# Time credited for the matrix engine's extra products, and convolution statistics that add on VectorE

## The chip, the cores and the metric

The kernel runs on one core of a Trainium2 chip. The metric is the device time of one execution in microseconds (us). The kernel before takes 1073.52 us, the median of three runs (1072.88 to 1074.54). Its engines are PE (TensorE, with the weight load PEld beside it), VectorE (DVE), ScalarE (ACT), GpSimd (POOL) and SyncE (SP), whose queue issues most transfers.

## The reference

Two layers of a decoder step for 288 tokens: 256 of a prompt and 32 of a sample (8 sequences of 4 tokens) that have a paged cache of 256 past positions. Everything is float32. One layer computes

```python
g_cols, u_pool, u_conf, u_sc, q, k, v, qi, ki, wi = split_cols(x @ w_in)
a_out = pool_mixer(u_pool)                                   # windowed means, group mix
cv = causal_dwconv(ga * sigmoid(gb), 31 taps) + conv_b       # 256 channels
b_out = silu(layer_norm(cv, conv_ln_g, conv_ln_b))           # mean and variance over channels
c_out = sb * causal_dwconv(sc_ * sh, 3 taps)
d_out = attend(rope(q), rope(k), v, rope(qi), rope(ki), wi)  # indexer scores, top-k, attention
gates = sigmoid(g_cols)                                      # four gates of 1024 channels
merged = sum of gates[i] * (branch_i @ w_br_i)
x1 = layer_norm(ALPHA * x + merged @ w_o)
r = ALPHA * x1 + (silu(hg) * hu) @ w_ffn_out                 # hg, hu = x1 @ w_ffn_in
y = layer_norm(r + (pe @ w_pe) * sigmoid(r @ w_pg))
```

The attention keeps, for each query, the 64 best keys by the indexer's score (relu of qi.ki, weighted by wi) and softmaxes over those.

## The kernel before

Activations lie feature-major, 128 features x 288 tokens. The weights are 2448 tiles of 128x128 that are streamed in 306 groups of 8. For each group a transfer brings 512 KB (wraw), ScalarE rounds them (whi, L264), VectorE subtracts (wlo = wraw - whi, L271), and each tile is used by three matmuls: whi by the high part of the activations, whi by the low part, wlo by the high part (L292 to L294; L318, L322 and L324 where several outputs grow side by side). A group keeps PE busy for 24 x 0.132 = 3.17 us. At the first tile of a group, `W` (L277) issues the rounding for the group three ahead and the subtraction for the group two ahead, and then calls `side` (L205): a tick.

Everything else of the mixers is side work: tasks written as generators (index_prompt, index_sample, attn_prompt, attn_sample, sconv, pool, conv). A tick gives each of two budgets, VectorE 1.96 us and ScalarE 2.3 us, on top of what was overdrawn:

```python
self.left[i] = min(self.left[i], 0.0) + self.budget[i]
```

Then ready tasks are stepped in turn while the budgets that they need are above zero. `yield d, a` takes declared times from the two budgets, `yield n` sleeps n ticks, and `yield VECTOR` or `BOTH` sets which budgets the task needs. The conv task is of low priority: it gets only what the others leave. Each engine executes in the order in which it was issued, so what a tick issues stands on VectorE behind one subtraction and ahead of the next. A product that a task issues on PE stands there between two weight groups, and nothing is debited or credited for its time.

PE's outputs go to two pools of four banks: `mm` for the projections, `ax` for the side work. After the q, k, v and short-conv projections come the pool projection, the gates 0 and 2 (one group per product; sigmoid on ScalarE, L1063), then the branches pool and sconv (two tiles per product, four products per group; VectorE multiplies by the gate, L1075 and L1078), then gates 1 and 3 and the branch of the attention. The side work runs in ticks 7 to 64 of layer 0 and 161 to 218 of layer 1; the branches pool and sconv start near tick 44 and 198.

The lines that matter later: conv's taps L684 (60 multiplies per layer), its products and reductions for the sample L690 and L693, its mean L704 and variance L714; index_prompt's copy of ki (L759), the two sleeps around it, its logits L777 and the top-k L748 and L752; the attention's logits L834, its Exp L851, the scaling by the reciprocal sum L858, transposes L870, output L882; index_sample's products L945 and L947 and its final mask addition L960; the pool mixer's L629 to L633.

Of the kernel before, what the change touches and what calls it, by code (L numbers as in the profile page):

```python
# [13 lines left out]
AF = mybir.ActivationFunctionType  # L14
# [100 lines left out]
class Builder:  # L115
# [103 lines left out]
    def cost(self, d, a):  # L219
        self.left[0] -= d  # L220
        self.left[1] -= a

    def finish(self, t):
        n = 0
# [445 lines left out]
    def conv(self):  # L670
        nc = self.nc
        ce, w = self.ce, self.par("conv_w")
        cv = yield from self.get_b([128, 2, N])
        bias = self.par("conv_b")
        es = [ce[:, c, 30 + TP:].rearrange("p (b w) -> p b w", b=NB) for c in range(2)]
        yield VECTOR
        for j in range(31):
            for c in range(2):
                wj = w[:, 31 * c + j:31 * c + j + 1]
                o, e = cv[:, c, :TP], ce[:, c, j:j + TP]  # L680
                if j == 0:
                    nc.vector.tensor_scalar(o, e, wj, bias[:, c:c + 1], op0=OP.mult, op1=OP.add)
                else:
                    nc.vector.scalar_tensor_tensor(o, e, wj, o, op0=OP.mult, op1=OP.add)  # L684
                yield 0.49, 0
        pr = yield from self.get_b([128, NB, TS, 31])
        for c in range(2):
            e = es[c]
            e = bass.AP(tensor=e.tensor, offset=e.offset, ap=[list(e.ap[0]), [34, NB], [1, TS], [1, 31]])
            nc.vector.tensor_tensor(pr, e, w[:, None, None, 31 * c:31 * c + 31].to_broadcast([128, NB, TS, 31]),  # L690
                                    op=OP.mult)
            yield 1.1, 0
            nc.vector.tensor_reduce(bt(cv[:, c, TP:]), pr, axis=AX.X, op=OP.add)  # L693
            yield 1.1, 0
            nc.vector.tensor_scalar(cv[:, c, TP:], cv[:, c, TP:], bias[:, c:c + 1], None, op0=OP.add)
            yield 0.1, 0
        yield BOTH
        self.free()
        self.free()
        yield 1  # L700
        mu, var = yield from self.get_ax(2)
        mu, var = mu[:, :N], var[:, :N]
        for c in range(2):
            nc.tensor.matmul(mu, self.c("o1024"), cv[:, c], start=c == 0, stop=c == 1)  # L704
        sq = [self.s(), self.s()]
        for c in range(2):
            nc.vector.scalar_tensor_tensor(cv[:, c], mu, -4.0, cv[:, c], op0=OP.mult, op1=OP.add)
            yield 0.4, 0
        for c in range(2):
            nc.scalar.activation(sq[c], cv[:, c], AF.Square)  # L710
        yield 0, 0.8
        yield 1
        for c in range(2):
            nc.tensor.matmul(var, self.c("o1024"), sq[c], start=c == 0, stop=c == 1)  # L714
        sd = self.s()
        nc.scalar.activation(sd, var, AF.Sqrt, bias=self.c("eps"), scale=4.0)
        yield 0, 2.0
        yield 1
        self.free_ax(2)
        rs = self.s()  # L720
        nc.vector.reciprocal(rs, sd)
        yield 2.0, 0
        g, b = self.par("cg"), self.par("cb")
        t = [self.s(), self.s()]
        for c in range(2):
            nc.vector.tensor_tensor(cv[:, c], cv[:, c], rs, op=OP.mult)
            yield 0.4, 0
        for c in range(2):
            nc.vector.tensor_scalar(cv[:, c], cv[:, c], g[:, c:c + 1], b[:, c:c + 1], op0=OP.mult, op1=OP.add)
            yield 0.4, 0  # L730
        for c in range(2):
            nc.scalar.activation(t[c], cv[:, c], AF.Sigmoid)
            yield 0, 0.45
        yield 1
        for c in range(2):
            nc.vector.tensor_tensor(cv[:, c], cv[:, c], t[c], op=OP.mult)
            yield 0.4, 0
        self.br["conv"] = yield from self.parts(cv)
# [17 lines left out]
    def index_prompt(self):  # L756
# [1 line left out]
        yield 2  # L758
        nc.scalar.activation(self.ki[64:], self.ki[:64], AF.Copy)  # L759
        yield 0, 0.33  # L760
        yield 2
        wp = self.sb.tile([128, 2, 4], F32, name="wp", tag="wp", bufs=1)
        a = yield from self.get_ax()
        for i in range(2):
# [5 lines left out]
        for i in range(2):  # L770
# [4 lines left out]
            for h in range(4):  # L775
                r = slice(64 * (h % 2), 64 * (h % 2) + 64)
                nc.tensor.matmul(a[h % 2][:, h // 2], self.qi[r, h // 2, 128 * i:128 * (i + 1)], self.ki[r, :n],  # L777
                                 start=True, stop=True)
            for e in range(2):
                nc.scalar.activation(rl[:, e::2], a[e], AF.Relu, scale=0.0625)  # L780
                yield 0, 0.3 + n / 600
# [19 lines left out]
    def attn_prompt(self):  # L801
# [5 lines left out]
        for i in range(3):  # L807
            rows = 128 if i < 2 else NS
            a = yield from self.get_ax()
            for c in range(4):  # L810
                nc.tensor.transpose(a[:rows, 128 * c:128 * (c + 1)], self.v[:, c, 128 * i:128 * i + rows], ident)
            nc.scalar.activation(vt[:, i] if i < 2 else vs, a[:rows], AF.Copy)
            self.free_ax()
            yield 0, 0.65
# [5 lines left out]
        for i in range(2):  # L820
# [6 lines left out]
            for h1 in range(0, 8, 2 * hb):  # L827
# [4 lines left out]
                for h in range(h1, h1 + 2 * hb):  # L832
                    r = slice(64 * (h % 2), 64 * (h % 2) + 64)
                    nc.tensor.matmul(a[h % 2][:, (h - h1) // 2], self.q[r, h // 2, 128 * i:128 * (i + 1)],  # L834
                                     self.k[r, h // 2, :n], start=True, stop=True)
                yield 1
                hs = slice(h1, h1 + 2 * hb)
                for e in range(2):
# [23 lines left out]
            for kc in range(i + 1):  # L862
                pt = yield from self.get_b([128, 8, 128])
                pts.append(pt)
                for h0 in range(0, 8, 4):
                    a = yield from self.get_ax()
                    v = a.rearrange("p (h q) -> p h q", h=4)
                    for h in range(h0, h0 + 4):
                        lg = lgs[h // (2 * hb)]
                        nc.tensor.transpose(v[:, h - h0], lg[:, hb * (h % 2) + h % (2 * hb) // 2,  # L870
                                                             128 * kc:128 * (kc + 1)], ident)
                    nc.scalar.activation(pt[:, h0:h0 + 4], v, AF.Copy)
                    self.free_ax()
                    yield 0, 0.65
# [4 lines left out]
            for c in range(4):  # L879
                for kc in range(i + 1):  # L880
                    for s in range(2):
                        nc.tensor.matmul(o[64 * s:64 * s + 64, c], vt[:, kc, 128 * c + 64 * s:128 * c + 64 * s + 64],  # L882
                                         pts[kc][:, 2 * c + s], start=kc == 0, stop=kc == i)
            self.free(len(pts))
            w = slice(128 * i, 128 * (i + 1))
            nc.scalar.activation(dp[0][:, :, w], o, AF.Copy)
# [41 lines left out]
    def index_sample(self):  # L928
# [15 lines left out]
        for p in range(4):  # L944
            nc.tensor.matmul(a[32 * p:32 * p + 32, :NK], self.qibd[:, p].rearrange("p r h t -> p (r h t)"),  # L945
                             self.kx[:, p], start=True, stop=True)
        nc.tensor.matmul(a[:, 288:288 + NS], self.c("hsel")[:4], self.wi[:, TP:], start=True, stop=True)  # L947
        rl = self.sb.tile([128, NK], F32, name="rls", tag="rls", bufs=1)
        nc.scalar.activation(rl, a[:, :NK], AF.Relu, scale=0.0625)
        yield 0, 0.4  # L950
# [4 lines left out]
        yield 2  # L955
        a = yield from self.get_ax()
        nc.tensor.matmul(a[:NS, :NK], ws, rl, start=True, stop=True)
        sc = self.sb.tile([NS, NK], F32, name="scs", tag="scs", bufs=1)
        nc.scalar.activation(sc[:, :TP], a[:NS, :TP], AF.Copy)
        nc.vector.tensor_tensor(sc[:, TP:], a[:NS, TP:NK], self.c("vb")[:NS], op=OP.add)  # L960
# [9 lines left out]
    def attn_sample(self):  # L970
# [12 lines left out]
        for f in range(2):  # L983
# [7 lines left out]
            for c in range(4):  # L991
                for j in range(4):
                    nc.tensor.matmul(a[32 * j:32 * j + 32, :NK],  # L993
                                     self.qbd[:, c, 4 * f + j].rearrange("p h t -> p (h t)"),
                                     kt[j][:, :, c], start=False, stop=c == 3)
            yield 1
            st = self.sb.tile([128, 3], F32, name="sts", tag="sts", bufs=2)
            nc.vector.tensor_reduce(st[:, 0:1], a[:, :NK], axis=AX.X, op=OP.max)
# [29 lines left out]
            for kc in range(2):  # L1028
                for j in range(4):
                    nc.tensor.matmul(a[32 * j:32 * j + 32], pt[:, kc, 32 * j:32 * j + 32], vc[j][:, kc].rearrange("p c k -> p (c k)"),  # L1030
                                     start=False, stop=kc == 1)
            m = yield from self.get_b([128, 512])
            nc.scalar.activation(m, a, AF.Copy, scale=st[:, 2:3])
            self.free_ax()
# [3 lines left out]
            for c in range(4):  # L1038
                nc.tensor.transpose(a[:, 128 * c:128 * (c + 1)], m[:, 128 * c:128 * (c + 1)], ident)
            self.free()  # L1040
            w = slice(TP + 16 * f, TP + 16 * f + 16)
            own = []
            for s in range(2):
# [432 lines left out]
```

## Time and profile before

| | |
|---|---|
| median of 3 runs | 1073.52 us |
| the profiled execution's own time | 1073.4 us |
| its span | 1071.5 us |
| PE busy | 1055.5 us, 98%, 8078 matmuls |
| VectorE busy | 763.2 us, 71%, 1319 instructions |
| ScalarE busy | 564.2 us, 53%, 950 instructions |
| GpSimd busy | 157.1 us, 15% |
| granted PE clock, mean | 0.997 of full speed (2.4 GHz) |
| read from memory | 182.49 MB, 175 GB/s with the writes |

The span is from the first to the last recorded instruction; 1.9 us of the execution lie outside it. PE is the engine that is nearly always busy. Matmuls are pipelined: a record of 0.29 us starts 0.13 us after the one before, so progress is read from start to start. Rows of a timeline can merge several instructions of a kind (x4).

### The profile page before, as it was taken

To read this page: it belongs to the slowest core of one execution; us is meant where nothing else is said; L and a number is where in the kernel's file an instruction comes from. 1 tells how busy PE (TensorE), PEld (TensorE's weight loads), DVE (VectorE), ACT (ScalarE), POOL (GpSimd) and SP (SyncE) were. 2 spreads that over 40 slices of the span, in tenths; PEclk is the share of its full clock that TensorE was granted. 3 is DMA by queue.
4 is the path that set the end of the run, shared out by engine and by line. 5 is a ranking of instruction groups with operands and counts; after the bars stand their busy time and mean duration, and the time that the engine had idled before them with its cause. 6 is when DMAs were issued, how large, how long until landed. Compare 5 with 4: busy or idle time off the path is not lost.

```text
span 1071.5 us, 20583 instructions
## 1 busy us (share of the span) xinstructions
PE 1055.5 (98%) x8078; PEld 1022.4 (95%) x8078; DVE 763.2 (71%) x1319; ACT 564.2 (53%) x950; POOL 157.1 (15%) x177
## 2 busy tenths in 40 slices
PE   9999999999999999999999999999999999999996
PEld 8999989899999999999999999898999999999996
DVE  5898869668785565544789888786688756555456
ACT  4886446554564444434578665554645644443344
POOL 0530003005500000000425100030055000000004
PEclk9999999999999999999999999999999999999998
DMA  8577646554455555544555766465453545554541
GB/s 304 168 247 213 201 144 227 197 167 147 150 164 172 157 171 168 174 157 169 161 183 164 264 190 216 122 225 205 139 169 128 186 158 170 171 171 159 171 143 45
DMA packets 61778, 188.57 MB, mean 176 GB/s; under 512 B 7602, under 2 KB 12274, under 8 KB 61682
## 3 DMA queue, kind: packets, MB, share of 16 engines
q1 hardware_dynamic: 60546, 183.55, 52.8%
q0 software_dynamic: 992, 3.57, 1.0%
q8 instruction: 63, 1.03, 0.4%
q14 instruction: 33, 0.27, 0.1%
q10 hardware_dynamic: 144, 0.15, 0.1%
HBM read 182.49 MB, written 4.75 MB: 175 GB/s over the span
## 4 chain that ended last, share of the span: by engine, by line
PE 90%; DVE 4%; ACT 2%; issue 1%; DMA 1%; POOL 1%; SPq 1%; POOLq 0%; DVEq 0%; ACTq 0%
PE mm L292 25%; PE mm L293 25%; PE mm L294 24%; PE mm L322 2%; PE mm L324 2%; PE mm L318 2%; DVE wlo L271 1%; DMA wraw<-in_w_dram 1%; POOL b L374 1%; PE ax L293 1%; PE ax L294 1%; PE ax L292 1%; DVE b L684 1%; PE ax L993 1%; PE ax L1030 1%
## 5 line engine op out<-in xcount | busy, mean ns | idle before, releaser
L271 DVE TENSOR_TENSOR wlo<-wraw,whi 128x1024 fp32r<-128x1024 f32 (+1 forms) x309 | 385.7, 1251 | 161.6 <-issue 80.8
L292 PE MATMUL mm<-xh,whi 128*128 128x288 f32 x1536 | 455.5, 297 | 1.0 <-DVE s L1078 1.0
L293 PE MATMUL mm<-xl,whi 128*128 128x288 f32 x1536 | 453.1, 295 | 0.0
L294 PE MATMUL mm<-xh,wlo 128*128 128x288 f32 x1536 | 452.9, 295 | 0.2 <-DVE wlo L271 0.2
L264 ACT ACTIVATE whi<-wraw 128x1024 fp32r<-128x1024 f32 (+1 forms) x309 | 322.7, 1047 | 160.8 <-PE mm L293 80.7
L292 PEld LDWEIGHTS mm<-xh,whi 128*128 128x128 f32 x1536 | 288.8, 188 | 9.3 <-issue 7.3
L294 PEld LDWEIGHTS mm<-xh,wlo 128*128 128x128 f32 x1536 | 288.6, 188 | 0.6 <-DVE wlo L271 0.6
L293 PEld LDWEIGHTS mm<-xl,whi 128*128 128x128 f32 x1536 | 288.8, 188 | 0.3
L292 PE MATMUL mm<-b,whi 128*128 128x288 f32 x576 | 171.5, 298 | 1.9 <-DVE m L1075 1.9
L293 PE MATMUL mm<-b,whi 128*128 128x288 f32 x576 | 169.9, 295 | 0.0
L294 PE MATMUL mm<-b,wlo 128*128 128x288 f32 x576 | 169.5, 294 | 0.0
L292 PEld LDWEIGHTS mm<-b,whi 128*128 128x128 f32 x576 | 107.9, 187 | 2.8 <-DVE m L1075 2.6
L294 PEld LDWEIGHTS mm<-b,wlo 128*128 128x128 f32 x576 | 108.5, 188 | 0.0
L293 PEld LDWEIGHTS mm<-b,whi 128*128 128x128 f32 x576 | 108.1, 188 | 0.2
L1079 POOL TENSOR_TENSOR m<-m,s 128x288 f32<-128x288 f32 x32 | 37.7, 1209 | 268.5 <-DVE s L1078 268.5
L343 POOL TENSOR_TENSOR b<-xf 128x288 f32<-128x288 f32 x4 | 4.9, 1215 | 443.0 <-DVE xf L1230 434.4
L1203 ACT ACTIVATE b<-s 128x288 fp32r<-128x288 f32 x44 | 19.2, 444 | 92.3 <-DVE s L1198 92.3
L684 DVE SCALAR_TENSOR_TENSOR b<-b,prm 128x256 f32<-128x256 f32 x120 | 58.9, 539 | 0.1
L1198 DVE TENSOR_TENSOR s<-s,mm 128x288 f32<-128x288 f32 x40 | 18.0, 454 | 50.6 <-PE mm L294 50.6
L1063 ACT ACTIVATE xf<-mm 128x288 f32<-128x288 f32 x32 | 13.2, 411 | 53.9 <-PE mm L294 53.8
L1063 ACT ACTIVATE g<-mm 128x288 f32<-128x288 f32 x32 | 13.2, 411 | 47.9 <-PE mm L294 47.8
L1206 DVE TENSOR_TENSOR b<-s,b 128x288 fp32r<-128x288 f32 x44 | 19.8, 457 | 19.4 <-ACT b L1203 19.4
(252 smaller groups left out, 1198.2 us busy)
## 6 DMA issues: line engine op xcount, KB each, us to landing
wraw<-in_w_dram SPq DMA_DIRECT2D x304, 512.0 KB, 3.5
kv<-in_ck_dram SPq DMA_DIRECT2D x32, 260.0 KB, 5.3
kv<-in_cv_dram SPq DMA_DIRECT2D x32, 256.0 KB, 5.2
out_ko_dram<-b POOLq DMA_DIRECT2D x2, 576.0 KB, 3.4
out_vo_dram<-b POOLq DMA_DIRECT2D x2, 576.0 KB, 5.8
kv<-in_kidx_dram SPq DMA_DIRECT2D x32, 32.0 KB, 2.8
b<-in_p_dram SPq DMA_DIRECT2D x3, 288.0 KB, 3.8
wraw<-in_w_dram SPq DMA_DIRECT2D x3, 256.0 KB, 5.3
```

What stands on the lines that cost most here:

```text
L264: self.nc.scalar.activation(self.hi[g][:, c[i]], self.raw[g][:, c[i]], AF.Copy)
L271: self.nc.vector.tensor_tensor(self.lo[g][:, c[i]], self.raw[g][:, c[i]], self.hi[g][:, c[i]].bitcast(F32), op=OP.subtract)
L292: m(out, wh, rh, start=first, stop=False)
L293: m(out, wh, rl, start=False, stop=False)
L294: m(out, wl, rh, start=False, stop=last)
L318: m(o, wh, rh[:, k], start=k == 0, stop=False)
L322: m(o, wh, rl[:, k], start=False, stop=not early and k == nk - 1)
L324: m(o, wl, rh[:, k], start=False, stop=False)
L684: nc.vector.scalar_tensor_tensor(o, e, wj, o, op0=OP.mult, op1=OP.add)
L1063: self.nc.scalar.activation(g, a, AF.Sigmoid)
L1079: nc.gpsimd.tensor_tensor(self.m[:, j], self.m[:, j], t, op=OP.add)
L1206: nc.vector.tensor_tensor(h[:, 1, i % 2], t, h[:, 0, i % 2].bitcast(F32), op=OP.subtract)
```

## The change

A method `gain` adds a time to both budgets. Tasks call it right after they have issued a product on PE, with a time in us. The conv's statistics add their two halves on VectorE first, so that one matmul gives the mean and one the variance, and the squares move from ScalarE to VectorE. The second sleep of index_prompt is three ticks instead of two.

```diff
+    def gain(self, t):
+        self.left[0] += t
+        self.left[1] += t
...
+        both = self.s()
+        nc.vector.tensor_tensor(both, cv[:, 0], cv[:, 1], op=OP.add)
+        yield 0.45, 0
...
-        for c in range(2):
-            nc.tensor.matmul(mu, self.c("o1024"), cv[:, c], start=c == 0, stop=c == 1)
+        nc.tensor.matmul(mu, self.c("o1024"), both, start=True, stop=True)
+        self.gain(0.25)
...
         for c in range(2):
-            nc.scalar.activation(sq[c], cv[:, c], AF.Square)
-        yield 0, 0.8
+            nc.vector.tensor_tensor(sq[c], cv[:, c], cv[:, c], op=OP.mult)
+            yield 0.45, 0
+        nc.vector.tensor_tensor(sq[0], sq[0], sq[1], op=OP.add)
+        yield 0.45, 0
         yield 1
-        for c in range(2):
-            nc.tensor.matmul(var, self.c("o1024"), sq[c], start=c == 0, stop=c == 1)
+        nc.tensor.matmul(var, self.c("o1024"), sq[0], start=True, stop=True)
+        self.gain(0.25)
...
         nc.scalar.activation(self.ki[64:], self.ki[:64], AF.Copy)
         yield 0, 0.33
-        yield 2
+        yield 3
...
```

The other calls stand behind these products (lines of before): the index logits L777 `gain(0.4 + n / 400)` with n = 128 and 256, the transposes of v `gain(0.4)` three times, the attention logits L834 `gain(1.1)`, the transposes L870 `gain(0.35)` for each four, the output L882 `gain(1.0 * (i + 1))` for query block i, index_sample's products L945 and L947 together `gain(1.2)` and its weighted sum `gain(0.6)`, the sample attention's logits L993 `gain(2.3)`, its output L1030 `gain(3.0)` and its transposes L1039 `gain(0.35)`.

After the change lines are numbered some 5 to 20 higher: L271 becomes L276, L684 L689, L748 L758, L752 L762, L785 to L791 L796 to L802, L690 and L693 L695 and L698, L695 L700, L834 L846, L851 L864, L858 L871, L870 L883, L952 L968, L960 L977, L1053 L1073, L1063 L1083, L1075 L1095.

How it moves instructions, at three places. VectorE in layer 0, around the subtraction for weight group 22, before: sc is the prompt's index score in the top-k, m a maximum.

```order
L271 TENSOR_TENSOR wlo<-wraw,whi 128x1024
L748 MAX m_1107<-sc 128x8
L752 MATCH_REPLACE sc<-m_1107,sc 128x256
L748 MAX m_1112<-sc 128x8
L752 MATCH_REPLACE sc<-m_1112,sc 128x256
L748 MAX m_1117<-sc 128x8
L271 TENSOR_TENSOR wlo<-wraw,whi 128x1024
L752 MATCH_REPLACE sc<-m_1117,sc 128x256
L748 MAX m_1163<-sc 128x8
```

The same place after; the last L276 is the subtraction for group 22, scs the sample's index score.

```order
L802 SCALAR_TENSOR_TENSOR sc<-const_214,sc 128x128
L758 MAX m_1077<-sc 128x8
L762 MATCH_REPLACE sc<-m_1077,sc 128x256
L276 TENSOR_TENSOR wlo<-wraw,whi 128x1024
L758 MAX m_1117<-sc 128x8
L762 MATCH_REPLACE sc<-m_1117,sc 128x256
L758 MAX m_1132<-sc 128x8
L762 MATCH_REPLACE sc<-m_1132,sc 128x256
L758 MAX m_1135<-sc 128x8
L276 TENSOR_TENSOR wlo<-wraw,whi 128x1024
L762 MATCH_REPLACE sc<-m_1135,sc 128x256
L977 TENSOR_TENSOR scs<-ax,const_214 32x4
```

Ahead of that subtraction (the second L271 before, the last L276 after) one more maximum and one more replace have been issued, and the sample's mask addition L977 stands right behind it, one replace later.

ScalarE in layer 0 at the end of gate 2, before: g is a gate's sigmoid, whi a rounded weight group, b,st the Exp of one head with its sum.

```order
L1063 ACTIVATE g<-mm 128x288
L264 ACTIVATE whi<-wraw 128x1024
L1063 ACTIVATE g<-mm 128x288
L264 ACTIVATE whi<-wraw 128x1024
L851 ACT_TABLE_LOAD
L851 ACTIVATE b,st<-b,st 128x256 x8
L264 ACTIVATE whi<-wraw 128x1024 x4
```

The same place after.

```order
L1083 ACTIVATE g<-mm 128x288
L269 ACTIVATE whi<-wraw 128x1024
L864 ACT_TABLE_LOAD
L864 ACTIVATE b,st<-b,st 128x256 x8
L1083 ACT_TABLE_LOAD
L1083 ACTIVATE g<-mm 128x288
L269 ACTIVATE whi<-wraw 128x1024
L1083 ACTIVATE g<-mm 128x288
L269 ACTIVATE whi<-wraw 128x1024 x5
```

The eight Exps with their table load moved ahead of the last two sigmoids of gate 2, and a second table load came between.

VectorE in layer 0 at the first products of the pool branch, before: m is the gated product.

```order
L684 SCALAR_TENSOR_TENSOR b<-b,prm 128x256 x4
L1075 TENSOR_TENSOR m<-mm,xf 128x288 x4
L271 TENSOR_TENSOR wlo<-wraw,whi 128x1024
L684 SCALAR_TENSOR_TENSOR b<-b,prm 128x256
L1075 TENSOR_TENSOR m<-mm,xf 128x288 x4
```

The same place after; b<-ax are the small subtractions of the sample's attention.

```order
L276 TENSOR_TENSOR wlo<-wraw,whi 128x1024
L700 TENSOR_SCALAR b<-b,prm 128x32
L695 TENSOR_TENSOR b<-b,prm 128x992
L1095 TENSOR_TENSOR m<-mm,xf 128x288 x4
L276 TENSOR_TENSOR wlo<-wraw,whi 128x1024
L1073 TENSOR_TENSOR b<-ax,b 64x4x16 x2
L698 TENSOR_REDUCE b<-b 128x32
L1095 TENSOR_TENSOR m<-mm,xf 128x288 x4
```

The conv's tap multiplies have left this place, and its product and reduction for the sample stand there now.

## Rows read from the trace of the kernel before

**Rows 1.** The page: busy us (share of the span) and instructions of each engine.

```profile
PE 1055.5 (98%) x8078; PEld 1022.4 (95%) x8078; DVE 763.2 (71%) x1319; ACT 564.2 (53%) x950; POOL 157.1 (15%) x177
```

**Rows 2.** Waits of PE: waited for, us in total, times, longest us.

```profile
PE mm L292 <- DVE m L1075: 1.9, 3, 0.9
PE ax L777 <- ACT ki L759: 1.0, 1, 1.0
PE mm L292 <- DVE s L1078: 1.0, 2, 0.6
```

**Rows 3.** Timeline of PE, layer 1, pool branch: start us, us, instruction, idle before.

```profile
695.57 0.29 PE L294 MATMUL mm<-b,wlo 128*128 128x288 f32 x1
696.80 0.41 PE L292 MATMUL mm<-b,whi 128*128 128x288 f32 x1 [0.94 <-DVE m L1075]
697.04 0.30 PE L293 MATMUL mm<-b,whi 128*128 128x288 f32 x1
```

**Rows 4.** Timeline of PE, layer 0, at the convolution's mean.

```profile
222.48 1.13 PE L704 MATMUL ax<-b,const 128*128 128x288 f32 x4
223.23 0.51 PE L292 MATMUL mm<-xh,whi 128*128 128x288 f32 x1
```

**Rows 5.** Timeline of VectorE, layer 1, pool branch.

```profile
701.30 1.54 DVE L1075 TENSOR_TENSOR m<-mm,xf 128x288 f32<-128x288 f32 x4
```

**Rows 6.** Timeline of VectorE, layer 0, the end of the convolution.

```profile
218.16 1.19 DVE L690 TENSOR_TENSOR b<-b,prm 128x992 f32<-128x992 f32 x1
219.38 1.19 DVE L693 TENSOR_REDUCE b<-b 128x32 f32<-128x992 f32 x1
...
226.88 1.23 DVE L271 TENSOR_TENSOR wlo<-wraw,whi 128x1024 fp32r<-128x1024 f32 x1 [2.07 <-issue]
```

**Rows 7.** Timeline of PE, layer 0, at the prompt's index logits.

```profile
42.09 0.49 PE L777 MATMUL ax<-ki,qi 64*128 64x128 f32 x2
43.61 0.71 PE L777 MATMUL ax<-ki,qi 64*128 64x128 f32 x6 [1.03 <-ACT ki L759]
```

**Rows 8.** Timeline of VectorE, layer 0, up to the subtraction for group 22.

```profile
68.93 0.87 DVE L684 SCALAR_TENSOR_TENSOR b<-b,prm 128x256 f32<-128x256 f32 x2
...
74.75 0.41 DVE L752 MATCH_REPLACE8 sc<-m,sc 128x256 f32<-128x256 f32 x1
75.19 0.43 DVE L748 MAX8 m<-sc 128x8 f32<-128x256 f32 x1
...
76.52 1.21 DVE L271 TENSOR_TENSOR wlo<-wraw,whi 128x1024 fp32r<-128x1024 f32 x1
```

**Rows 9.** Timeline of PE, layer 0, ahead of weight group 21.

```profile
78.76 0.65 PE L945 MATMUL ax<-kv,qibd 128*32 128x260 f32 x8
...
79.67 1.16 PE L834 MATMUL ax<-b 64*128 64x128 f32 x16
```

**Rows 10.** Timeline of PE, layer 0, the first matmul of weight group 33.

```profile
119.70 0.29 PE L292 MATMUL mm<-xh,whi 128*128 128x288 f32 x1
```

**Rows 11.** Timeline of VectorE, layer 0, scalings between pool operations.

```profile
120.90 1.22 DVE L271 TENSOR_TENSOR wlo<-wraw,whi 128x1024 fp32r<-128x1024 f32 x1
122.04 0.28 DVE L858 TENSOR_SCALAR b<-b,st 128x128 f32<-128x128 f32 x1
...
123.18 0.29 DVE L858 TENSOR_SCALAR b<-b,st 128x128 f32<-128x128 f32 x1
```

**Rows 12.** Timeline of ScalarE, layer 1, the Exp block among gate 2's sigmoids.

```profile
690.34 0.41 ACT L1063 ACTIVATE g<-mm 128x288 f32<-128x288 f32 x1 [1.81 <-PE mm L294]
690.64 1.05 ACT L264 ACTIVATE whi<-wraw 128x1024 fp32r<-128x1024 f32 x1
691.72 1.28 ACT L851 ACT_TABLE_LOAD   x1
...
697.08 1.28 ACT L1063 ACT_TABLE_LOAD   x1
698.37 0.41 ACT L1063 ACTIVATE g<-mm 128x288 f32<-128x288 f32 x1
```

More of the change, by code (lines that the diff above doesn't have):

```diff
@@ L778, in index_prompt @@
                                  start=True, stop=True)
+            self.gain(0.4 + n / 400)
             for e in range(2):
@@ L811, in attn_prompt @@
                 nc.tensor.transpose(a[:rows, 128 * c:128 * (c + 1)], self.v[:, c, 128 * i:128 * i + rows], ident)
+            self.gain(0.4)
             nc.scalar.activation(vt[:, i] if i < 2 else vs, a[:rows], AF.Copy)
@@ L835, in attn_prompt @@
                                      self.k[r, h // 2, :n], start=True, stop=True)
+                self.gain(1.1)
                 yield 1
@@ L871, in attn_prompt @@
                                                              128 * kc:128 * (kc + 1)], ident)
+                    self.gain(0.35)
                     nc.scalar.activation(pt[:, h0:h0 + 4], v, AF.Copy)
@@ L883, in attn_prompt @@
                                          pts[kc][:, 2 * c + s], start=kc == 0, stop=kc == i)
+            self.gain(1.0 * (i + 1))
             self.free(len(pts))
@@ L947, in index_sample @@
         nc.tensor.matmul(a[:, 288:288 + NS], self.c("hsel")[:4], self.wi[:, TP:], start=True, stop=True)
+        self.gain(1.2)
         rl = self.sb.tile([128, NK], F32, name="rls", tag="rls", bufs=1)
@@ L957, in index_sample @@
         nc.tensor.matmul(a[:NS, :NK], ws, rl, start=True, stop=True)
+        self.gain(0.6)
         sc = self.sb.tile([NS, NK], F32, name="scs", tag="scs", bufs=1)
@@ L995, in attn_sample @@
                                      kt[j][:, :, c], start=False, stop=c == 3)
+            self.gain(2.3)
             yield 1
@@ L1031, in attn_sample @@
                                      start=False, stop=kc == 1)
+            self.gain(3.0)
             m = yield from self.get_b([128, 512])
@@ L1040, in attn_sample @@
             self.free()
+            self.gain(0.35)
             w = slice(TP + 16 * f, TP + 16 * f + 16)
```

## The prediction

> **What bounds the kernel now.** I read the page's busy line first, then the waits of TensorE (PE), then the timeline of one engine at a time around each wait. PE is busy for 98% of the span, VectorE for 71%, ScalarE for 53% [rows 1], so a stretch ends when PE has got through its products, unless PE has to stop. Where it stops is in the list of its waits: in the branch products for VectorE's gate multiplies (2.9 us in five stops) and once, in layer 0, at the index logits L777 for a ScalarE copy [rows 2]. The other entries of that list (start-up, layer norms) lie in code that the change leaves alone. A stop costs more than its entry: where the list has 0.94, the first matmul after it starts 1.23 us after the one before instead of 0.13, and the next comes after 0.24 instead of 0.13 [rows 3], so 1.21 us, 0.27 more than listed. Five such stops cost 2.9 + 5 x 0.27 = 4.2 us.
>
> The change does two things. It takes matmuls from PE, and it lets more side work into each tick in which PE has an extra product. That side work runs on VectorE and ScalarE, in front of the weight subtraction (wlo), the gate sigmoids and the gate multiplies, all of which PE waits for. So I price three things: what PE no longer does, where VectorE falls behind, and where the Exp block of the prompt attention comes to stand.
>
> **1. Matmuls removed: -1.5 us.** The mean and the variance each lose one of two matmuls, in two layers: 4 matmuls. The two matmuls of L704 are four passes in the trace, and the weight tile after them starts 0.75 us after their first [rows 4]. Half of it is 0.375 us; four times that is 1.5 us, all on PE's path. In return VectorE gets two additions and two squarings per layer, on 128x288. Four gate multiplies of that size take 1.54 us [rows 5], so this is some 1.5 us more per layer on VectorE and 0.8 less on ScalarE. I cost it at nothing: it stands behind the conv's last reductions, where VectorE sits idle for some 2 us between two subtractions [rows 6]. Without that cover it would be 3.0 us in both layers.
>
> **2. The stop at L777: -1.1 us.** PE does two passes at 42.09 and the other six at 43.61, with 1.03 us idle [rows 7]. The third tick of sleep puts these products a group later, about 3.2 us, when the copy is done. The gap is 1.5 us from start to start, of which two passes are 0.2: 1.3 goes at most. Nothing else is in front of PE there but the subtraction; I take 1.1, with 0.5 and 1.3 as ends, since VectorE is late in that stretch and loses the time that PE's stop gave it.
>
> **3. VectorE's lag in layer 0: +4.7 us, in two places.** The first is the prompt attention's first logits, L834 (L846 after), in the tick of PE's group 21. Counted in the two orders up to the subtraction for group 22, VectorE has done four more conv multiplies (two take 0.87 overlapped, so 0.40 each), one more maximum (0.43), one more replace with its value load (0.5) and a small multiply (0.1): 2.6 us. That subtraction starts at 76.52 now [rows 8], hence at about 79.2. One replace stands between it and L977, the addition that frees the bank for these logits: 79.2 + 1.13 + 0.5 + 0.1 gives 81.0. PE is there at 78.76, less 1.1 from step 2, plus the 0.9 of the sample's index products that now come earlier [rows 9]: 78.6. It stops for 2.4 us. At present the same logits wait for nothing. The ends are 1 and 4: one conv multiply more or less is 0.4, and the subtraction itself varies with the copies it waits for.
>
> The second place is the transposes L870 (L883 after), now two ticks behind their scalings, after the change one. VectorE stands 1.2 us behind when PE begins group 33 (119.70 against 120.90) [rows 10, 11]. After the stop above it is 0.4 behind (79.2 plus a round of 3.4, against PE at 82.2; a round is 1.14 for the subtraction, the budget of 1.96 and some 0.3 of overdraft); the credits of 1.1 and 0.6 add 1.7, and eleven rounds that are each about 0.1 longer than PE's 3.17 add 1.2: 3.3 us. Behind the subtraction (1.14) stand a scaling with a set of pool operations, 1.14 together [rows 11], and the second scaling that the transposes need. So they can start at 3.3 + 1.1 + 1.1 = 5.5 us after PE began the group; PE is there after 3.2. That is 2.3 us, with 0.4 (lag as now) and 3.5 as ends.
>
> In layer 1 the L777 stop does not occur (its count is 1 [rows 2]); side work starts there with a VectorE that is not behind. The tick counts give two ticks to the transposes. I take 0.6 us for the first place, between 0 and 1.5.
>
> **4. The gate sigmoids and the branch: +4.0 us.** Now the Exp block of the second query block stands behind all sigmoids of gate 2 in layer 0 and before the last one in layer 1. After the change it stands before the last two, in both layers. The block with its two table loads fills ScalarE from 691.72 to the next sigmoid at 698.37, 6.65 us, and that sigmoid starts 8.03 us after the one ahead of the block [rows 12].
>
> PE has four banks for these products. With its start of the second-last gate product as zero: the sigmoid before the block starts at about 0.16, the second-last at 8.2, and it ends at 8.6. PE ends both gate products at 6.3 and two branch products (six matmuls each, 0.79) at 7.9; the third needs the bank of that sigmoid: 0.75. ScalarE then rounds a weight group (1.05 [rows 12]) and does the last sigmoid by 9.96, for which the fourth product stops 0.4. The rounded group lets VectorE start the subtraction at 9.6; behind it stand a short bias addition and a conv multiply of 1.19 [rows 6], and the first gate multiply ends at 12.5, where the fifth product stops from 10.85: 1.67. One round later two small subtractions and a conv reduction of 1.19 [rows 6] hold the next multiplies to 16.6, against PE at 15.75: 0.85. Sum 3.7, with 0.11 for each of four restarts 4.1 per layer, 8.2 in both. Less the 4.2 there now, that is +4.0. Ends: +2.5 (the last 0.85 gone in both layers) and +5.5 (each stop 0.2 longer).
>
> On the table loads the trace shows the load of 1.28 us at 697.08 and the sigmoid at 698.37, with no gap [rows 12]. The Trainium skill ("ScalarE: Activation LUTs", section "What ACT_TABLE_LOAD costs") adds a drain of about 1.38 us to each switch. By it both sigmoids would come 1.38 us later per layer, an estimate of 2.8 us more; this trace disagrees, and I leave it out.
>
> **The sum.** The profiled execution took 1073.4 us (span 1071.5, and 1.9 around it), 0.1 below the median of 1073.52. 1073.4 - 1.5 - 1.1 + 2.4 + 2.3 + 0.6 + 4.0 = **1080.1 us**. With its terms at the ends that most likely go together, this case runs from 1076 to 1084.
>
> **Rivals.** *Only PE counts (faster).* The place is the branch stretch of both layers and the tick of the first logits; the mechanism is that PE's own extra products, now declared, really are time in which VectorE works, so that it is nowhere late. For it: VectorE is idle 29% of the span [rows 1], and the conv multiplies that stand in front of the branch multiplies now (four, then one, in the excerpt) are done earlier after the change. It decides at the bank of the first stop: if the second-last sigmoid is done before 7.9 us in the count above (it comes at 8.6), and the subtraction for group 22 starts before 76.8, nothing is added and steps 1 and 2 are left: 1073.4 - 2.6 = 1070.8 us; without the stops there now, down to 1066.6. Against it: both orders put the block before the sigmoids, and 6.65 us is read from the trace. The Trainium skill ("Perfetto Trace Analysis", section "Identifying the Most-Contended Engine") says to improve the most contended engine first; by that rule alone PE's 2.6 us would be the result, and this trace agrees that PE is that engine.
>
> *Branch only (no change to slightly slower).* VectorE catches up in layer 0, as it does now after every long product, and only step 4 stands: 1073.4 - 2.6 + 4.0 = 1074.8 us. For it: the list of waits has no stop at L834 or L870 now, and VectorE's lag of 1.2 us at group 33 [rows 10, 11] is far from stopping PE. Against it: the excerpts show the bank of the first logits now freed by an operation behind the subtraction.
>
> *Lag only.* The branch costs what it costs now (the multiplies catch up within the four banks), and VectorE's lag remains: 1073.4 - 2.6 + 5.3 = 1076.1 us; with the two stops halved, 1073.4.
>
> **How the numbers follow.** No change means within 0.2%, 1071.4 to 1075.7 us, about what a measurement of this kernel can tell. The forecast has 0.58, all slower. Only PE counts: 0.14, of it 0.10 faster and 0.04 the same. Branch only: 0.16, 0.10 the same and 0.06 slower. Lag only: 0.12, 0.04 the same and 0.08 slower. So faster 0.10, same 0.18, slower 0.72. The range of 1073.0 to 1083.5 leaves out most of the first rival and the forecast's far end, about 0.2.
>
> **What would show it.** Right: the list of PE's waits has the first attention logits waiting for VectorE's addition L977 once, the transposes for the scalings once, and the branch products in each layer about 4 us, the first of them for a sigmoid on ScalarE; L777 is gone; L704's successor shows two passes. The prediction is wrong if the branch products' waits stay near 2.9 us in sum, or if VectorE's subtraction for group 22 starts before 77: then the credit was cover, as the first rival has it. It is also wrong if the waits are as foretold and the span is not longer, for then PE gets the time back elsewhere.

## The result, and the profile after

The changed kernel took 1079.22 us, the median of four runs (1078.86 to 1080.01), against 1073.2 us (1072.44 to 1074.54) for the kernel before beside it. The ratio is 1.0055 (95% interval 1.0043 to 1.0067): 6 us slower. The forecast was 1080.1. The profiled execution's span went from 1071.5 to 1077.1 us, 5.6 more.

PE still bounds the kernel. These are the first eight lines of its waits after, which answer to [rows 2] (columns as there).

```profile
PE mm L297 <- DVE m L1095: 4.7, 4, 1.5
PE ax L960 <- ACT kv L955: 1.7, 1, 1.7
PE mm L297 <- ACT g L1083: 1.6, 4, 0.6
PE ax L431 <- DVE q L426: 1.0, 1, 1.0
PE ax L1286 <- PEq L1401: 0.8, 1, 0.8
PE ax L402 <- DVE xf L1250: 0.7, 1, 0.7
PE mm L299 <- DVE wlo L276: 0.5, 1, 0.5
PE ax L883 <- DVE b L871: 0.5, 1, 0.5
```

The branch products now have eight stops, 4.7 us for VectorE's multiplies and 1.6 us for sigmoids on ScalarE, where before they had five with 2.9 us. L777 is gone from the list. L960, the sample's index products, is new and was not forecast, and so is the stop of 0.5 us for the subtraction at L299; L431, L1286 and L402 belong to code that is as before.

The timeline of PE at the pool branch of layer 0 has the four stops one after the other (start us, us, instruction, idle before). Layer 1 has the same four.

```profile
167.66 0.40 PE L297 MATMUL mm<-b,whi 128*128 128x288 f32 x1 [0.60 <-ACT g L1083]
168.91 0.40 PE L297 MATMUL mm<-b,whi 128*128 128x288 f32 x1 [0.18 <-ACT g L1083]
171.49 0.40 PE L297 MATMUL mm<-b,whi 128*128 128x288 f32 x1 [1.52 <-DVE m L1095]
175.79 0.40 PE L297 MATMUL mm<-b,whi 128*128 128x288 f32 x1 [0.85 <-DVE m L1095]
```

By [rows 3] a stop costs 0.16 us more than its idle time up to the matmul that waited and 0.11 us at the next. Read up to the matmul that waited, they are 0.76, 0.34, 1.68 and 1.01 us; the count ahead of the run had 0.75, 0.4, 1.67 and 0.85.

ScalarE beside them, the end of the Exp block and the two sigmoids behind it; this answers to [rows 12].

```profile
160.54 1.28 ACT L864 ACT_TABLE_LOAD   x1
...
165.90 1.28 ACT L1083 ACT_TABLE_LOAD   x1
167.20 0.41 ACT L1083 ACTIVATE g<-mm 128x288 f32<-128x288 f32 x1
167.50 1.05 ACT L269 ACTIVATE whi<-wraw 128x1024 fp32r<-128x1024 f32 x1
168.45 0.40 ACT L1083 ACTIVATE g<-mm 128x288 f32<-128x288 f32 x1
```

From the block's first load to the first sigmoid it is 6.66 us, as the 6.65 of before, and the load is again followed by the sigmoid without a gap. VectorE in the same stretch:

```profile
168.59 1.23 DVE L276 TENSOR_TENSOR wlo<-wraw,whi 128x1024 fp32r<-128x1024 f32 x1 [2.25 <-ACT whi L269]
169.73 0.23 DVE L700 TENSOR_SCALAR b<-b,prm 128x32 f32<-128x32 f32 x1
169.88 1.19 DVE L695 TENSOR_TENSOR b<-b,prm 128x992 f32<-128x992 f32 x1
170.98 1.54 DVE L1095 TENSOR_TENSOR m<-mm,xf 128x288 f32<-128x288 f32 x4
```

The subtraction waits 2.25 us for the rounding that stood behind the block, and the conv's product takes 1.19 us between it and the first multiply. So two things hold the multiply, the late rounding and the conv's product, and the runs below take them apart.

The first matmul of the mean after, against [rows 4]:

```profile
197.79 0.75 PE L711 MATMUL ax<-s,const 128*128 128x288 f32 x2
198.17 0.51 PE L297 MATMUL mm<-xh,whi 128*128 128x288 f32 x1
```

Two passes, 0.38 us to the next weight tile; the variance takes 0.27. Four passes had taken 0.75 each time, so a layer saves 0.85 us.

### The profile page after: what moved, and what is told of

It is laid out like the page before. It is cut to its first block, busy times and chain, and to the rows that moved or that the text cites. A ratio compares the mean times of both kernels' runs of the same rounds, so it can differ in the third digit from the quotient of the medians.

```text
span 1077.1 us, 20572 instructions
## 1 busy us (share of the span) xinstructions
PE 1057.1 (98%) x8070; PEld 1023.0 (95%) x8070; DVE 766.1 (71%) x1327; ACT 561.2 (52%) x946; POOL 159.4 (15%) x177
## 4 chain that ended last, share of the span: by engine, by line
PE 90%; DVE 4%; ACT 3%; issue 1%; POOL 1%; DMA 1%; SPq 0%; POOLq 0%; ACTq 0%; DVEq 0%
PE mm L297 24%; PE mm L298 24%; PE mm L299 24%; PE mm L327 2%; PE mm L329 2%; PE mm L323 2%; DVE wlo L276 1%; POOL b L379 1%; PE ax L298 1%; PE ax L299 1%; PE ax L297 1%; ACT whi L269 1%; PE ax L329 1%; PE ax L327 1%; PE ax L1010 1%
## 5 line engine op out<-in xcount | busy, mean ns | idle before, releaser
L276 DVE TENSOR_TENSOR wlo<-wraw,whi 128x1024 fp32r<-128x1024 f32 (+1 forms) x309 | 384.0, 1245 | 153.1 <-PE mm L299 67.3
L299 PE MATMUL mm<-xh,wlo 128*128 128x288 f32 x1536 | 453.0, 295 | 0.6 <-DVE wlo L276 0.5
L299 PEld LDWEIGHTS mm<-xh,wlo 128*128 128x128 f32 x1536 | 288.6, 188 | 1.1 <-DVE wlo L276 1.0
L299 PE MATMUL mm<-b,wlo 128*128 128x288 f32 x576 | 169.5, 294 | 0.0
L299 PEld LDWEIGHTS mm<-b,wlo 128*128 128x128 f32 x576 | 108.5, 188 | 0.0
L1099 POOL TENSOR_TENSOR m<-m,s 128x288 f32<-128x288 f32 x32 | 36.2, 1157 | 268.7 <-DVE s L1098 268.7
L689 DVE SCALAR_TENSOR_TENSOR b<-b,prm 128x256 f32<-128x256 f32 x120 | 59.4, 553 | 0.0
L1083 ACT ACTIVATE g<-mm 128x288 f32<-128x288 f32 x32 | 13.1, 411 | 55.9 <-PE mm L299 55.9
L1083 ACT ACTIVATE xf<-mm 128x288 f32<-128x288 f32 x32 | 13.1, 410 | 42.2 <-PE mm L299 41.9
```

The lines of the kernel that those rows point to most:

```text
L276: self.nc.vector.tensor_tensor(self.lo[g][:, c[i]], self.raw[g][:, c[i]], self.hi[g][:, c[i]].bitcast(F32), op=OP.subtract)
L299: m(out, wl, rh, start=False, stop=last)
L1083: self.nc.scalar.activation(g, a, AF.Sigmoid)
L1099: nc.gpsimd.tensor_tensor(self.m[:, j], self.m[:, j], t, op=OP.add)
```

## The experiments

Each time is a median beside runs of the kernel before on the same chip (1072.7 to 1073.4 us); the ratio is to those.

**Conv statistics alone.** The kernel before with the statistics of the diff, without `gain` and with `yield 2`.

> The kernel before with the convolution statistics of the change alone (sum of the halves on VectorE, one matmul each for mean and variance, squares on VectorE), no credit, no longer sleep. Theory (the four matmuls lie on PE's path and the added VectorE work is covered): 1.5 us faster than before, two passes instead of four at the mean and at the variance, stops elsewhere unchanged. Rival (VectorE's four operations per layer delay the subtraction that follows them): no change, or up to 1.5 us slower, with PE waiting for wlo behind them.

1072.08 us, ratio 0.9989 (0.998 to 0.9998), so 1.3 us faster. The gain is small but clear; the list of PE's waits shows none around the statistics. The matmuls were on the path, and the work added to VectorE is covered where it stands. One stop is new, 0.3 us in layer 1 behind the conv's own branch product; the sleep alone has it as well, so it is not of the statistics alone.

**The change without the statistics.** The changed kernel with the old two matmuls and Squares.

> The changed kernel with the convolution statistics of before; the credits and the third tick of sleep stay. Theory: 1.5 us slower than the changed kernel, so some 7.5 us above before, with the branch products' stops as in the changed kernel (idle 2.4 for VectorE and 0.8 for ScalarE in each layer). Rival (the statistics' extra VectorE work is what makes the branch late): the stops at the branch shrink to those of before, and it is faster than the changed kernel.

1081.12 us, 1.0069 (1.0056 to 1.0083), 1.9 above the changed kernel's median (1.5 by the two ratios). The branch stops are those of the changed kernel (2.4 and 0.8 us in layer 0). The statistics do not cause them.

**Exp block after the branches.**

```diff
             yield 1
+            while i == 1 and not self.branched:
+                yield 1
             for h in range(8):
                 lg = lgs[h // (2 * hb)][:, h % (2 * hb)]
                 nc.scalar.activation(lg, lg, AF.Exp, ...
```

`branched` is set once both branches have been issued.

> The changed kernel, but the Exp block of the second query block is held until both branches have been issued; credits, sleep and statistics stay. Theory (the block ahead of the last two sigmoids causes the stops at the branch): the sigmoids come on time, the two ScalarE stops vanish and the first two multiplies' stops with them; 8.3 us of stops in both layers shrink to 0 to 2, so 6 to 8 us faster than the changed kernel, 1071 to 1073. Rival (the conv operations ahead of the gate multiplies cause them): the ScalarE stops of 0.8 a layer vanish, the VectorE stops of 2.4 a layer stay; 2 us faster.

1074.44 us, 1.0009 (1.0 to 1.0018): 4.8 us faster than the changed kernel, less than the 6 to 8 expected. Two lines of its waits say why.

```profile
PE mm L297 <- DVE m L1097: 2.8, 4, 1.1
PE ax L962 <- ACT kv L957: 1.7, 1, 1.7
```

No stop for a sigmoid is left, and VectorE's stops fell from 4.7 to 2.8 us. The rest looks like the rival's: conv operations stand ahead of the multiplies. The next run tests that.

**Conv out of the branches as well.** On top of the last one, low-priority tasks are not stepped while the branches are issued:

```diff
-            ready = [t for t in self.tasks if can(t)]
+            ready = [t for t in self.tasks if can(t) and not (t.low and self.keep_low)]
```

> The changed kernel with credits, with the Exp block of the second query block held until both branches have been issued, as in the run with the late Exp block, and besides with no convolution operation issued while the branches are. Theory (the stops that the late Exp block left, 1.4 us idle per layer, are the convolution's product and reduction ahead of the gate multiplies): they go, 3.5 to 4 us faster than with the late Exp block alone, 1070.5 to 1071. Rival (the first multiplies are late for another reason, as the subtraction's own time): 1074.

1071.32 us, 0.998 (0.9971 to 0.9989), 3.1 us faster again, a little less than expected. All eight branch stops are gone from its list; L963's 1.7 us (L960 in the changed kernel) is now its longest wait. So the branch's cost has two causes, the Exp block with some 4.8 us and the conv's operations with 3.1, for stops that came to 8.5 us in the trace (idle time and restarts). The two holds also clear what the branches had cost before the change.

**The sample's index products a tick later.** The changed kernel, with `yield 2` instead of `yield 1` ahead of L960.

> The changed kernel with index_sample's first products L960 one tick later; everything else as in the changed kernel. Theory (the credit lets ScalarE's copies be issued in the tick just ahead of the products, and PE stops for them and then pays each further wait of these four matmuls): the stop of 1.7 us in layer 0 is gone, and the products take 0.58 us again instead of 1.20 in both layers; 3.1 us faster if VectorE's lag does not take it back. Rival (VectorE's lag): that stop was the time in which VectorE caught up; without it the subtraction, the first logits or the transposes stop PE for 1 to 2 us more in layer 0, so 1 to 2 us faster. Third (the four products are slower for another reason, as their place among weight groups): 1.20 us stays.

1079.91 us, 1.0059 (1.0046 to 1.0073): no faster. But the thing it was made for happened. First PE in the changed kernel, then in this run:

```profile
68.64 1.27 PE L960 MATMUL ax<-kv,qibd 128*32 128x260 f32 x8 [1.66 <-ACT kv L955]
69.84 0.40 PE L962 MATMUL ax<-wi,const 4*128 4x32 f32 x2
```

```profile
70.95 0.65 PE L960 MATMUL ax<-kv,qibd 128*32 128x260 f32 x8
71.53 0.40 PE L962 MATMUL ax<-wi,const 4*128 4x32 f32 x2
```

The stop is gone, and the products take 0.58 us to the next start instead of 1.20. What ate it is in the branch, where three of the conv's operations (reduction, bias, product) now stood ahead of the multiplies: one stop of 2.86 us, and the granted PE clock of the stretches around it (us; busy times of the engines, then PEclk, DMA share, GB/s):

```profile
170.93 0.61 PE L297 MATMUL mm<-b,whi 128*128 128x288 f32 x1 [2.86 <-DVE m L1095]
```

```profile
165.00:170.00 5.00, 2.29 (x14) 1.67 (x12) 3.27 (x4) 3.95 (x6) 0.00 (x0) 1.00 0.24 75
170.00:173.00 3.00, 2.07 (x8) 2.08 (x9) 2.97 (x6) 0.00 (x0) 0.00 (x0) 0.52 0.23 89
173.00:176.00 3.00, 3.00 (x14) 3.00 (x14) 2.27 (x5) 0.00 (x0) 0.00 (x0) 0.50 0.49 175
176.00:180.00 4.00, 4.00 (x29) 4.00 (x28) 2.89 (x6) 1.06 (x1) 0.87 (x2) 0.88 0.10 13
```

After idling, PE ran at the lower of its two levels (a granted clock of 0.50, 1.2 GHz) for some 6 us, with matmuls 0.24 us apart instead of 0.13: 2.6 us lost besides the stop. Layer 1 had the same stop (2.85 us) with some 3.5 us at 0.50, 1.4 us lost. All five executions of this kernel show a mean clock of 0.992 or 0.993. No expectation had this.

**The same without that stop.** Exp block and conv out of the branches, and the products a tick later.

> The changed kernel with credits, Exp block and convolution held out of the branches as before, and index_sample's first products one tick later, as in the run with the late products, where a stop of 3 us in the branch and a PE clock at half speed after it hid what that gave. Theory (the stop for ScalarE's copies and the four products' extra 0.62 us per layer are real losses): 2 to 3 us faster than with only the two holds (1071.3), 1068.3 to 1069.3. Rival (VectorE's lag takes the place of that stop): less than 1 us faster, with PE waiting for the subtraction or the transposes in layer 0.

1067.21 us, 0.9947 (0.9934 to 0.9961): 4.1 us faster than with the two holds alone by the medians, 3.5 by the ratios, more than expected. It is the lowest median here, but its interval overlaps those of the kernels without credit below. The waits left are those of the code that nothing touched, and 0.4 and 0.2 us in layer 0:

```profile
PE ax L432 <- DVE q L427: 1.0, 1, 1.0
PE ax L1293 <- PEq L1408: 0.8, 1, 0.8
PE ax L403 <- DVE xf L1257: 0.7, 1, 0.7
PE mm L300 <- DVE wlo L277: 0.4, 1, 0.4
PE mm L324 <- ACT xh L447: 0.4, 1, 0.4
PE ax L330 <- DVE wlo L277: 0.3, 1, 0.3
PE ax L899 <- DVE b L657: 0.2, 1, 0.2
```

The stop for ScalarE's copies was a real loss, and VectorE's lag did not take its place; the stop at the transposes went too.

**Credit for VectorE alone.** `gain` without its second line.

> The changed kernel with the credit given to VectorE's budget alone, none to ScalarE's. By the order of instructions the Exp block then stands ahead of one sigmoid of gate 2 in each layer, not two. Theory (what the branch costs goes with the number of sigmoids behind the block: 1.4 us for none and 2.8 for one in the kernel before, 4.2 for two in the changed one): about 1.4 us less in each layer, 1076 to 1077. Rival (VectorE's load alone sets it): the branch's stops stay as in the changed kernel, 1079. The stop at the sample's products stays for both.

1080.13 us, 1.0057 (1.0044 to 1.007): as slow as the changed kernel, so the rival's time, for a reason that neither had. The branch's idle time did fall, to 1.9 us in layer 0 and 2.4 in layer 1 from 3.2 in each. But layer 0's is one stop, behind which the clock was again at 0.50 for some 3 us (1.5 us lost), and the pool mixer's products now wait for VectorE, 0.4 us in layer 0 and 0.8 in layer 1. Waits and clock in layer 0:

```profile
PE ax L647 <- DVE b L637: 0.4, 1, 0.4
...
PE mm L296 <- DVE m L1094: 1.9, 1, 1.9
```

```profile
168.00:171.00 3.00, 1.06 (x8) 0.90 (x7) 2.71 (x6) 2.97 (x9) 0.00 (x0) 0.95 0.80 285
171.00:174.00 3.00, 3.00 (x14) 3.00 (x14) 2.40 (x3) 1.97 (x3) 0.00 (x0) 0.50 0.03 5
```

The stop at the sample's products stayed at 1.7 us. As a test of the count of sigmoids it is inconclusive: the order of the conv moved as well.

**Third tick of sleep alone.** The kernel before with `yield 3`.

> The kernel before with the third tick of sleep in index_prompt alone. Theory (the stop at L777 is a stop of PE that nothing else takes the place of): the stop is gone, 1.1 to 1.5 us faster than before, 1072 to 1072.3. Rival (PE only meets VectorE's late subtraction instead, since that stop gave VectorE time): PE waits for wlo or for the index products' operands nearby, and the time is that of before.

1070.19 us, 0.9967 (0.9954 to 0.998): 2.9 us, twice what was expected. The stop at L777 went, and with it three of the five branch stops, as the sleep moved the side work behind it (0.9 and 0.4 us in layer 1 are left). Some 1.5 us are the stop's; the rest came with the order, in which the branch stops cost 1.9 us (idle and restarts) where they had cost 4.2.

**Statistics and sleep, no credit.**

> The changed kernel without any credit: the kernel before with the convolution statistics of the change and the third tick of sleep. Theory (the two parts add up: 1.3 us for the statistics and 2.9 for the sleep as run by themselves, and the credits alone make the change slow): 1068.5 to 1069.3, so the credits cost some 10 us. Rival (without credit the statistics' extra VectorE work meets the sleep's shifted work): 1070 or more.

1068.0 us, 0.9956 (0.9943 to 0.997), what the two parts give one by one. The changed kernel is this one plus the credits, at a ratio of 1.0055 to the same base: the credits cost 1.0055 - 0.9956 = 0.0099, or 10.6 us, give or take 2. The spans (1065.8 and 1077.1) differ by 11.3. The branch stops of this run are two, both in layer 1:

```profile
PE mm L292 <- DVE m L1078: 1.4, 2, 0.9
```

With restarts they cost 1.9 us, where the changed kernel's cost 8.5. So by the traces the branches are 6.6 us of the credits' cost, the stop and the slower products at L960 3.0 (1.8 and 1.2), the subtraction and the transposes 1.3; a few tenths either way lie elsewhere. In this run's layer 0 the Exp block still stands behind all sigmoids of gate 2, and no branch product waits.

**Other ways to use the holds without credit.** Statistics and sleep with the late Exp block and the conv held; then the same with the conv free.

> No credit: the kernel before with the convolution statistics of the change, the third tick of sleep, the Exp block of the second query block held until both branches have been issued, and no convolution operation issued while they are. Theory (PE's time plus its stops): 1073.4 less 1.5 for the statistics, 1.1 to 1.5 for the stop at L777 and 4.2 for the branches: 1066 to 1067. Rival (held side work comes back later in gates 1 and 3 as stops of the same size): 1070 or more, with new stops between the branches and the attention's branch.

1068.71 us, 0.9955 (0.9942 to 0.9967). The branch stops are gone, but in layer 1 PE stops 2.1 us for the copy (L1166) behind the gate multiply of the conv's own branch. VectorE does the held conv's last operations there and comes late to that multiply:

```profile
PE mm L319 <- ACT b L1166: 2.1, 1, 2.1
```

> No credit: statistics, third tick of sleep, and the Exp block held until both branches have been issued; convolution operations are free to stand in the branches (held in the earlier run, where the convolution then ended too late in layer 1 and PE stopped 2.1 us for it). Theory (what was lost there came from holding the convolution): that stop is gone, layer 1's branch stops of the sleep run (0.9 and 0.4 idle) too: 1066 to 1067.5. Rival (the convolution's taps ahead of the gate multiplies stop PE as much): 1068.5.

1068.32 us, 0.9953 (0.9939 to 0.9966), no better than without the late Exp block. That stop is down to 0.4 us, as in the kernel without any hold, and the branch stops of layer 1 are gone, but the sconv multiplies stop PE for 0.6 us in layer 0. The subtraction stops it for 0.7 at 36.2 us as well; the hold does not reach that far ahead, and the same stop is 0.2 us in the kernel before and 0.7 in the run with the late sample products. Both expectations were too good.

## Why the prediction came out right, and where its steps were wrong

The time was right to 0.9 us. Where the span's 5.6 us come from, step by step from the profile after:

| step | forecast | found |
|---|---|---|
| 1, matmuls removed | -1.5 | -1.7 |
| 2, stop at L777 | -1.1 | -1.5 |
| 3, VectorE's lag in layer 0 | +4.7 | +1.3 (subtraction 0.7, transposes 0.6) |
| not forecast: ScalarE late at L960, layer 0 | 0 | +1.8 |
| not forecast: L960's products, both layers | 0 | +1.2 |
| 3, layer 1 | +0.6 | 0 |
| 4, branches | +4.0 | +4.3 |
| not forecast: lower clock in the last matmuls | 0 | +0.7 |
| a stop of before for the subtraction that went | 0 | -0.5 |

These sum to 5.6. Steps 1, 2 and 4 hold, with the mechanism and nearly the size. Step 2 had 1.3 us as the most that could go; it was 1.5, for all eight passes together take 0.64 us to the next weight tile, as long as the last six had taken. Step 4 counts idle time plus 0.27 for each stop, as the prediction did: 6.3 + 8 x 0.27 = 8.5, less 4.2. That the Exp block is behind it and not only beside it is shown by the run that held it (-4.8), and that the conv's operations carry the rest by the run that held them too (-3.1). The 4.2 that step 4 takes off are another matter: the sleep alone brings them to 1.9, so the +4.3 is 6.6 us from the credits (8.5 less 1.9) less 2.3 that the sleep gave (4.2 less 1.9). The count needed no such split, since it went from one order to the other. The run with the lone statistics confirms step 1, the sleep alone step 2.

Step 3 named the wrong place. It set the first logits to stop 2.4 us for L977, the sample's mask addition on VectorE. VectorE was where the step had it, PE was not:

```profile
79.50 1.21 DVE L276 TENSOR_TENSOR wlo<-wraw,whi 128x1024 fp32r<-128x1024 f32 x1
80.62 0.08 DVE L762 MATCH_VALUE_LOAD sc<-m,sc 128x8 f32 x1
80.69 0.41 DVE L762 MATCH_REPLACE8 sc<-m,sc 128x256 f32<-128x256 f32 x1
81.02 0.14 DVE L977 TENSOR_TENSOR scs<-ax,const 32x4 f32<-32x4 f32 x1
```

L977 was forecast to end at 81.0 and ended at 81.16. PE was forecast there at 78.6 and came at 81.9, for it had stopped at 59.36 for the subtraction, then 1.66 us at L960, and had taken 0.6 us longer over those products. So the first logits waited for nothing. The step followed VectorE's queue through this stretch and not ScalarE's. In the kernel before ScalarE does the sample's ten copies in three ticks; with the credit they are issued in two, next to the products that need them:

```profile
66.40 1.05 ACT L269 ACTIVATE whi<-wraw 128x1024 fp32r<-128x1024 f32 x1
67.47 0.66 ACT L950 ACTIVATE qibd<-qi 64x16 f32<-64x16 f32 x3
68.15 0.44 ACT L955 ACTIVATE kv<-ki 64x16 f32<-64x16 f32 x2
```

The last copy ends at 68.59, and PE starts at 68.64. It is not ScalarE's share of the credit that moves them: this task is stepped only while both budgets are above zero, and with credit for VectorE alone the ten copies stand in the same two ticks, with the same stop of 1.66 us. The size of layer 0's lag came out near (3.1 found with the stop at L960, 4.7 forecast) because a PE that stops early for one engine gives the other time; that is luck in part. The second place, the transposes, did stop, for 0.6 us instead of 2.3. VectorE's lag there was 1.8 us (PE began the group at 118.02, the subtraction at 119.81), where the step had summed credits and rounds to 3.3; the step also takes a round once as 3.4 us and once as 0.1 longer than PE's 3.17.

Of the rivals, "only PE counts" is refuted for this change: with the credits, what the statistics and the sleep give is more than spent. It describes the change without its credits: 1068.0 lies between its 1070.8 and its 1066.6, since the sleep also removed branch stops. "Branch only" and "lag only" each had half of the truth.

## What to carry to other kernels

A product that the bounding engine has to compute anyway does not by itself make room on the others: work let in on its account is queued ahead of whatever the bounding engine needs next. It is the order that costs, not the credit as such: with the Exp block and the conv out of the branches and the sample's products a tick later, the kernel with credits takes 1067.2 us, and the one without takes 1068.0, which their intervals do not tell apart. When a planner's budget is raised, look for the places where the bounding engine has few buffers (four banks here) and read the order of every other engine there, ScalarE's copies as well as VectorE's sums. A change made of three parts is to be timed by parts: here two of them gave 5 us and the third cost 10.6.

## What was not expected of the hardware

Four matmuls of 128x32 into four groups of 32 partitions of one bank (L945, L960) take 0.58 us together when PE finds their operands ready, and run side by side: in the kernel before they start within 0.02 us. When the first had to wait, each of the others came 0.21 to 0.23 us after the one before, and the four took 1.20 us. In layer 1 the first was a mere 0.18 us late, and the products still took 1.20, so it is not the length of the wait. The trace has 18 semaphore waits at this line in the kernel before, in the changed kernel and in the run a tick later, where they cost nothing. That in the changed kernel they are taken one after the other is an inference from the starts.

In four places amid the weight products a stop was followed by PE at half its clock: 2.86 and 2.85 us idle with the sample's products a tick later, 1.94 us with credit for VectorE alone, and 2.12 us in layer 1 with the conv held and no credit, where the granted clock was 0.50 from 781 to 784 us. Each took 1.4 to 2.6 us more than the stop. Behind the longest stop of the changed kernel, 1.52 us, the clock stayed at full in the profiled execution, whose mean is 0.996; two of its other three have 0.993, so it may have fallen there. In the profile of the changed kernel the last eight small matmuls of the program (L431) took 1.98 us where the same eight took 1.11 before, at a mean granted clock of 0.75 over those 6 us; it took 1.98 again with credit for VectorE alone and with the conv held and no credit, 1.38 with the sample's products a tick later, and 1.11 or 1.23 in the eight other runs here. That covers the 0.7 us at the end, and it goes with none of the edits that these runs tell apart.
